# A fourth gate product with a wide moving operand, wide matmuls ahead of narrow ones, and eight slots traded for four wide buffers

## The chip, the cores and the metric

The kernel runs on one core of a Trainium2 chip. The metric is the device time of one execution in microseconds. Three runs of the kernel before took 1026.03, 1027.26 and 1027.35 us (median 1027.26).

## The reference

A decoder trunk of two layers on 512 tokens of width 1024 in float32. The first layer mixes with a gated short convolution, the second with sliding-window attention over one shared K/V; both end in a gated FFN of width 2816, and every part has a norm ahead and behind.

```python
def swiglu(h, w_gate_up, w_down):
    g, u = jnp.split(h @ w_gate_up, 2, axis=-1)
    return (jax.nn.silu(g) * u) @ w_down
...
kv = rmsnorm(h, kv_norm) @ w_kv
q = (rmsnorm(h, b_pre_norm[j]) @ b_w_q[j]).reshape(bsz, s, N_HEADS, HEAD_DIM)
attn = sliding_window_sink_attention(q, k_sh, v_sh, b_sinks[j]) @ b_w_o[j]
h = h + rmsnorm(attn, b_post_norm[j])
ff = swiglu(rmsnorm(h, ffn_pre_norm[l]), ffn_w_gate_up[l], ffn_w_down[l])
h = h + rmsnorm(ff, ffn_post_norm[l])
```

Attention has 16 heads of 64, 4 K/V heads, blocks of 128 queries that see their own and the previous block, and a sink logit per head.

## The kernel before, in words

**Precision.** Every float32 operand is kept as a rounded part (names ending in hi, made by ACT) and a rest (lo, made by DVE as the operand minus its rounded part). A product is three matmuls: hi times lo, hi times hi, lo times hi (`mm3`, L190 to L193). A weight tile of 128x1024 arrives by DMA as `raw`, ACT makes `whi` (L469), DVE makes `wlo` (L470); `in_line` (from L474) prepares them two jobs ahead of the job that uses them.

**Gate stage of an FFN.** `gate_jobs` (from L976) computes the gate and up projections of two feature tiles by seven block products in place of eight, in Strassen's manner, 10 groups of features per layer. The sums of token blocks are made once per layer in `factors` (L364), those of weight blocks by DMA accumulation or, for 6 of the 10 groups (`ADDED`), partly by DVE at L457. The products of a group run in the order 1, 2, 6, 5, 7, 3, 4. Products 1, 6, 7, 4 accumulate in one chain, X, of two banks (one for each half e of the outputs); 5 and 3 in chain Z, 2 in chain Y. After each product `take` (from L1001) copies or adds the banks into the buffers `st` and `u`.

For products 6, 7 and 4 the token factor `xt` is one wide buffer, its rounded part in columns 0 to 511 and its rest in 512 to 1023. A view of both pieces (256 columns of each) is one moving operand of 512 columns: one wide matmul (L1048) makes hi times hi into the bank's left half and hi times lo into its right half, and a narrow one (L1050, 256 columns) adds lo times hi on the left. They alternate: wide, narrow, wide, narrow, over e and k. The right half is added later by DVE (L1008). Product 1 takes the token tiles 0 to 3 themselves, whose two parts lie in separate slots, so it has three narrow matmuls per step and only a left half.

**Buffers.** One ring of 43 slots (`slot`: 128x512) and one of 14 wide buffers (`wide`: 128x1024) hold everything that is not a weight. `halves` gives the two halves of a wide buffer. A slot is handed out again in order; whoever writes its new tile waits for the last reader of the old one. Weights have 7 raw and 4 pairs of rounded buffers of their own.

**Order.** All four engines run what is written, in the order written (`manual_schedule`). In the attention stage the table `ORDER` sets it: per pair of heads t it interleaves scores, maxima, exponents, turning (transposing probabilities on PE), high (`phi`, ACT, L1369) and low (`plo`, DVE, L1373) parts of turned blocks, weighing (PE, `po`), the output `out` (L1389 to 1391), and the projection and rotation of the next heads' queries (`ra`, `rhi`, `rlo` at L1241, L1246, L1247; additions on POOL, which is GpSimd, for most). Scores, turned parts and rotated queries all live in slots. Ahead of it stands the projection of K and V from `xkv`, whose eight token tiles are split by `Update.split` (L338), as are the FFN's. An `Update` can have several sets of tiles n: the K/V update has n = 0 (for K and V) and n = 1 (for the queries), the FFN's only n = 0.

Of the kernel before, what the change touches and what calls it, by code (L numbers as in the profile page):

```python
# [11 lines left out]
F32R = mybir.dt.float32r  # L12
# [4 lines left out]
P = 128  # L17
D = 1024
S = 512
KT = D // P  # L20
# [31 lines left out]
    "L": "low", "W": "weigh", "O": "out", "Q": "project", "R": "rotate", "H": "split",  # L52
    "G": "weights", "Z": "project", "z": "out",
}
N_SLOT, N_WIDE, N_RAW, N_W = 43, 14, 7, 4
EARLY = 4
HD = 64
NH = 16
# [14 lines left out]
def yoco_kernel(  # L73
# [22 lines left out]
    nc = tc.nc  # L96
# [142 lines left out]
    class Update:  # L239
# [3 lines left out]
        def __init__(self, mix, gain, gpres):  # L243
            self.mix, self.gpres, self.gain = mix, gpres, gain
            self.s, self.v, self.r = (
                small.tile([P, n], F32, tag=tag, name=name(tag))
                for tag, n in (("us", 12), ("uv", 8), ("ur", 8))
            )
            self.x = [[None] * KT for _ in gpres]
            self.xn, self.banks, self.parts = {}, {}, {}  # L250
            self.leaves = False

        def load(self, queue=nc.sync):
# [82 lines left out]
                                        ident)  # L336

        def split(self, n, f, hf):  # L338
            if self.x[n][f] is None:
                self.x[n][f] = (slot("xhi", F32R), slot("xlo", F32R))  # L340
            hi, lo = self.x[n][f]
            c = slice(hf * 256, (hf + 1) * 256)
            src = self.banks[f % 4, hf][:, (f // 4) * 256 : (f // 4 + 1) * 256]
            nc.scalar.activation(hi[:, c], src, AF.Copy, scale=g(self.gpres[n], f))
            nc.vector.scalar_tensor_tensor(
                out=lo[:, c], in0=src, scalar=g(self.gpres[n], f), in1=hi[:, c].bitcast(F32),
                op0=ALU.mult, op1=ALU.subtract,
            )
# [15 lines left out]
        def factors(self):  # L364


            x = self.x[0]
            made = {p: [] for p in range(1, 8)}
            for p, k0, c in ((1, 0, 0), (2, 4, 0), (3, 4, 256)):
                made[p] = [[a[:, c : c + 256] for a in x[k0 + k]] for k in range(4)]  # L370
            for j in range(2):
                q11, q21, q12, q22 = (self.parts[i, hf, j] for hf in range(2) for i in range(2))

                nc.vector.tensor_tensor(out=q11, in0=q11, in1=q12, op=ALU.subtract)
                nc.vector.tensor_tensor(out=q12, in0=q22, in1=q12, op=ALU.subtract)
# [13 lines left out]
            return made  # L389
# [565 lines left out]
    def ffn(l, before, ahead, gain, gpres, following):  # L955
# [20 lines left out]
        def gate_jobs(q, factors, out, to, then):  # L976
# [24 lines left out]
            def take(p):  # L1001
                x, y, z = (banks.get(c) for c in "XYZ")
                st, u, gr = kept
                g0, g1 = (gr.rearrange("p (e h c) -> p e h c", e=2, h=2)[:, :, h]
                          for h in range(2))

                def add(out, a, b):
                    nc.vector.tensor_tensor(out=out, in0=a, in1=b, op=ALU.add)  # L1008

                if p == 2:  # L1010
                    add(g0, tiles(y), tiles(st))
                elif p == 5:
                    nc.scalar.activation(u, z, AF.Copy)
                elif p == 3:
                    add(g1, tiles(z), tiles(st))
                else:
                    for e in range(2):
                        a, b = x[e][:, :256], x[e][:, 256:]
                        ste, ue = (v[:, e * 256 : (e + 1) * 256] for v in (st, u))
                        if p == 7:  # L1020
# [3 lines left out]
                        nc.scalar.activation(ste, a, AF.Copy)  # L1024
                        if p != 1:
                            add(ste, b, ste)
                if p == 4:
                    for g, m in ((g0, st), (g1, u)):
                        nc.vector.scalar_tensor_tensor(out=g, in0=tiles(m), scalar=-1.0, in1=g,
                                                       op0=ALU.mult, op1=ALU.mult)  # L1030

            def run(p):
                def products(job):
# [5 lines left out]
                    if opened:  # L1039
                        banks[c] = ([bank("gx", pools[c]) for _ in range(2)] if c == "X"  # L1040
                                    else bank("g" + c.lower(), pools[c]))
                    for e in range(2):
                        for k in range(4):
                            kk = slice(e * S + k * P, e * S + (k + 1) * P)
                            xhi, xlo, *xboth = factors[p][k]
                            kw = {"skip_group_check": True}
                            if c == "X" and xboth:
                                nc.tensor.matmul(banks[c][e], whi[:, kk], xboth[0], start=False,  # L1048
                                                 stop=False, **kw)
                                nc.tensor.matmul(banks[c][e][:, :256], wlo[:, kk], xhi,  # L1050
                                                 start=False, stop=k == 3 and p == 4, **kw)
                                continue
                            out = (banks[c][e][:, :256] if c == "X"
                                   else banks[c][:, e * 256 : (e + 1) * 256])
                            mm3(out, whi[:, kk], wlo[:, kk], xhi, xlo,
                                opened and k == 0 and (c == "X" or e == 0),
                                e == 1 and k == 3 and p in (2, 3), **kw)
                    take(p)
                return products
# [213 lines left out]
    class Heads:  # L1273
# [343 lines left out]
```

## Time and profile before

| | |
|---|---|
| runs | 1026.03, 1027.26, 1027.35 us |
| profiled execution | 1026.46 us, of which span 1024.7 us |
| granted clock of PE | 0.999 |
| DVE add of a bank half (L1008) | 420 ns, 160 times |
| weight rounding on ACT (L469), rest on DVE (L470) | 1051 and 1227 ns, 225 times each |

In a timeline row the first number is the start in us from the span's start, the second the duration, then engine, line, operation, output and inputs, shape and count; a bracket gives the idle time of the engine ahead of it and what ended it. Matmuls are pipelined, so their durations overlap, and distances between starts say how fast the stream runs. A group row ends in busy time, mean of one in ns, and idle time ahead.

### The profile page before, as it was taken

To read this page: it belongs to the slowest core of one execution; us is meant where nothing else is said; L and a number is where in the kernel's file an instruction comes from. 1 tells how busy PE (TensorE), PEld (TensorE's weight loads), DVE (VectorE), ACT (ScalarE), POOL (GpSimd) and SP (SyncE) were. 2 spreads that over 40 slices of the span, in tenths; PEclk is the share of its full clock that TensorE was granted. 3 is DMA by queue.
4 is the path that set the end of the run, shared out by engine and by line. 5 is a ranking of instruction groups with operands and counts; after the bars stand their busy time and mean duration, and the time that the engine had idled before them with its cause. 6 is when DMAs were issued, how large, how long until landed. Compare 5 with 4: busy or idle time off the path is not lost.

```text
span 1024.7 us, 16538 instructions
## 1 busy us (share of the span) xinstructions
PE 1015.1 (99%) x6168; PEld 900.3 (88%) x6168; DVE 858.7 (84%) x1440; ACT 582.3 (57%) x1035; POOL 196.9 (19%) x259
## 2 busy tenths in 40 slices
PE   9999999999999999999999999999999999999997
PEld 8888888999889898998897888889998998989986
DVE  5766767889789988989869998778997898889896
ACT  7323445865655454666476776677666554645641
POOL 0443033112111111000123653232111010110001
PEclk9999999999999999999999999999999999999999
DMA  9897689459979699879504779976899576998742
GB/s 357 288 266 225 184 255 350 136 167 292 348 238 296 195 305 307 267 210 318 170 5 160 187 229 277 254 264 153 270 289 328 167 245 226 299 298 249 240 149 82
DMA packets 66576, 244.52 MB, mean 239 GB/s; under 512 B 7872, under 2 KB 8384, under 8 KB 54720
## 3 DMA queue, kind: packets, MB, share of 16 engines
q1 hardware_dynamic: 51328, 145.98, 38.9%
q0 software_dynamic: 14592, 96.48, 36.9%
q8 instruction: 48, 0.79, 0.3%
q10 hardware_dynamic: 576, 1.02, 0.3%
q14 instruction: 32, 0.26, 0.1%
HBM read 237.15 MB, written 102.76 MB: 332 GB/s over the span
## 4 chain that ended last, share of the span: by engine, by line
PE 85%; DVE 8%; ACT 2%; DMA 2%; issue 2%; POOL 0%; DVEq 0%; ACTq 0%
PE gx L1048 10%; PE gx L1050 5%; PE pcub L191 4%; PE pcub L192 4%; PE pcub L193 4%; PE gz L193 3%; PE gz L192 3%; PE gz L191 3%; PE px L191 3%; PE px L193 3%; PE px L192 3%; PE pmix L191 2%; PE pmix L192 2%; PE pmix L193 2%; DMA raw<-in_w_gb_dram 2%; PE gy L193 2%
## 5 line engine op out<-in xcount | busy, mean ns | idle before, releaser
L470 DVE TENSOR_TENSOR wlo<-raw,whi 128x1024 fp32r<-128x1024 f32 x225 | 274.8, 1227 | 64.5 <-ACT whi L469 64.1
L469 ACT ACTIVATE whi<-raw 128x1024 fp32r<-128x1024 f32 x225 | 234.0, 1051 | 104.8 <-DVE raw L457 22.3
L1048 PE MATMUL gx<-xt,whi 128*128 128x512 f32 x480 | 172.5, 399 | 0.1
L1050 PE MATMUL gx<-xt,wlo 128*128 128x256 f32 x480 | 135.0, 281 | 0.0
L1048 PEld LDWEIGHTS gx<-xt,whi 128*128 128x128 f32 x480 | 90.4, 188 | 19.7 <-DVE st L1008 0.3
L538 POOL DMA_DIRECT2D hsum<-in_w_gb_dram x96 | 63.7, 751 | 143.9 <-ACT whi L469 82.6
L1050 PEld LDWEIGHTS gx<-xt,wlo 128*128 128x128 f32 x480 | 90.9, 189 | 0.1
L1024 ACT ACTIVATE st<-gx 128x256 f32<-128x256 f32 x120 | 43.0, 379 | 63.1 <-PE gx L1050 47.8
L538 POOL DMA_DIRECT2D hsum<-hsum x32 | 25.3, 790 | 258.9 <-ACT whi L469 192.0
L1008 DVE TENSOR_TENSOR st<-gx,st 128x256 f32<-128x256 f32 x160 | 62.9, 420 | 4.3 <-ACT st L1024 2.9
L192 PE MATMUL pcub<-xhi,whi 128*128 128x512 f32 x168 | 65.4, 389 | 0.0
L191 PE MATMUL pcub<-xlo,whi 128*128 128x512 f32 x168 | 65.4, 389 | 0.0
L193 PE MATMUL pcub<-xhi,wlo 128*128 128x512 f32 x168 | 65.4, 389 | 0.0
L1062 ACT ACTIVATE gr<-gr 128x1024 f32<-128x1024 f32 x20 | 21.3, 1065 | 49.2 <-DVE gr L1008 49.2
L191 PE MATMUL px<-wlo,ahi 128*128 128x512 f32 x120 | 46.8, 390 | 0.1
L192 PE MATMUL px<-whi,ahi 128*128 128x512 f32 x120 | 46.7, 389 | 0.0
L193 PE MATMUL px<-whi,alo 128*128 128x512 f32 x120 | 46.7, 389 | 0.0
L193 PE MATMUL gz<-xhi,wlo 128*128 128x256 f32 x160 | 45.4, 284 | 0.0
L191 PE MATMUL gy<-xlo,whi 128*128 128x256 f32 x160 | 45.3, 283 | 0.0
L192 PE MATMUL gy<-xhi,whi 128*128 128x256 f32 x160 | 45.3, 283 | 0.0
L193 PE MATMUL gy<-xhi,wlo 128*128 128x256 f32 x160 | 45.3, 283 | 0.0
L192 PE MATMUL gx<-xhi,whi 128*128 128x256 f32 x160 | 45.3, 283 | 0.0
(265 smaller groups left out, 3064.5 us busy)
## 6 DMA issues: line engine op xcount, KB each, us to landing
hsum<-in_w_gb_dram POOLq DMA_DIRECT2D x96, 512.0 KB, 7.9
raw<-hsum SPq DMA_DIRECT2D x88, 512.0 KB, 7.6
raw<-in_w_gb_dram SPq DMA_DIRECT2D x60, 512.0 KB, 7.6
hsum<-in_w_dn_dram POOLq DMA_DIRECT2D x36, 512.0 KB, 8.8
raw<-in_w_dn_dram SPq DMA_DIRECT2D x32, 512.0 KB, 6.0
hsum<-hsum POOLq DMA_DIRECT2D x28, 512.0 KB, 5.9
raw<-in_w_in_dram SPq DMA_DIRECT2D x21, 512.0 KB, 7.8
hsum<-in_w_dn_dram POOLq DMA_DIRECT2D x12, 768.0 KB, 12.8
```

Source lines behind the costliest of these rows:

```text
L191: nc.tensor.matmul(out, whi, xlo, start=start, stop=False, **kw)
L192: nc.tensor.matmul(out, whi, xhi, start=False, stop=False, **kw)
L193: nc.tensor.matmul(out, wlo, xhi, start=False, stop=stop, **kw)
L469: self.begun = nc.scalar.activation(hi[:, :n], raw, AF.Copy)
L470: nc.vector.tensor_tensor(out=lo[:, :n], in0=raw, in1=hi[:, :n].bitcast(F32), op=ALU.subtract)
L538: nc.gpsimd.dma_start(dst, src, max_dma_last_dim=4 * 4 * S, **kw))
L1008: nc.vector.tensor_tensor(out=out, in0=a, in1=b, op=ALU.add)
L1024: nc.scalar.activation(ste, a, AF.Copy)
L1048: nc.tensor.matmul(banks[c][e], whi[:, kk], xboth[0], start=False, stop=False, **kw)
L1050: nc.tensor.matmul(banks[c][e][:, :256], wlo[:, kk], xhi, start=False, stop=k == 3 and p == 4, **kw)
L1062: nc.scalar.activation(kept[2], kept[2], AF.Silu)
```

## The change

Three things, in one edit.

1. **Product 1 with a wide operand.** `Update.split` puts token tiles 0 to 3 of set n = 0 in wide buffers; the view of both pieces goes to `factors` as a third entry of product 1. Product 1 then runs as 6, 7 and 4 do, and `take` adds its right half on DVE as well.
2. **Order in a job of chain X.** All 8 wide matmuls (both e, four k) come first, then all 8 narrow ones.
3. **Pools.** 35 slots and 18 wide buffers. The first four token tiles of the convolution, those of K/V and of both FFNs, and the first four outputs of attention move to halves of wide buffers.

```diff
-N_SLOT, N_WIDE, N_RAW, N_W = 43, 14, 7, 4
+N_SLOT, N_WIDE, N_RAW, N_W = 35, 18, 7, 4
+BOTH = 4
...
         def split(self, n, f, hf):
+            if self.x[n][f] is None and n == 0 and f < BOTH:
+                two = wide("xhl", F32R)
+                self.x[n][f] = two[:, :S], two[:, S:]
+                self.both[f] = two.rearrange("p (i c) -> p i c", i=2)
             if self.x[n][f] is None:
                 self.x[n][f] = (slot("xhi", F32R), slot("xlo", F32R))
...
             for p, k0, c in ((1, 0, 0), (2, 4, 0), (3, 4, 256)):
-                made[p] = [[a[:, c : c + 256] for a in x[k0 + k]] for k in range(4)]
+                made[p] = [[a[:, c : c + 256] for a in x[k0 + k]]
+                           + [two[:, :, c : c + 256] for two in self.both[k0 + k :][:1] if two]
+                           for k in range(4)]
...
-    xs = [(slot("xhi", F32R), slot("xlo", F32R)) for _ in range(KT)]
+    xs = [halves("xhl", F32R) if k < BOTH else (slot("xhi", F32R), slot("xlo", F32R))
+          for k in range(KT)]
...
                         nc.scalar.activation(ste, a, AF.Copy)
-                        if p != 1:
-                            add(ste, b, ste)
+                        add(ste, b, ste)
...
-                    for e in range(2):
-                        for k in range(4):
-                            kk = slice(e * S + k * P, e * S + (k + 1) * P)
-                            xhi, xlo, *xboth = factors[p][k]
-                            kw = {"skip_group_check": True}
-                            if c == "X" and xboth:
-                                nc.tensor.matmul(banks[c][e], whi[:, kk], xboth[0], start=False,
-                                                 stop=False, **kw)
-                                nc.tensor.matmul(banks[c][e][:, :256], wlo[:, kk], xhi,
-                                                 start=False, stop=k == 3 and p == 4, **kw)
-                                continue
...
+                    if c == "X":
+                        for e, k, kk in steps:
+                            nc.tensor.matmul(banks[c][e], whi[:, kk], factors[p][k][2],
+                                             start=opened and k == 0, stop=False, **kw)
+                        for e, k, kk in steps:
+                            nc.tensor.matmul(banks[c][e][:, :256], wlo[:, kk], factors[p][k][0],
+                                             start=False, stop=k == 3 and p == 4, **kw)
...
         def out(self):
-            hi, lo = slot("ohi", F32R), slot("olo", F32R)
+            if self.t < BOTH:
+                hi, lo = halves("ohl", F32R)
+            else:
+                hi, lo = slot("ohi", F32R), slot("olo", F32R)
```

PE has 160 matmuls fewer, DVE 40 additions more.

**PE, end of product 4 of one gate group and start of product 1 of the next** (`gx` is a bank of chain X, `xt` a token factor, `xhi`, `xlo` and `xhl` token tiles). Before:

```order
1114 L1048 MATMUL gx_2024<-xt_1899,whi_2150 128x512
1115 L1050 MATMUL gx_2024<-xt_1899,wlo_2151 128x256
1116 L1048 MATMUL gx_2024<-xt_1915,whi_2150 128x512
1117 L1050 MATMUL gx_2024<-xt_1915,wlo_2151 128x256
1118 L1048 MATMUL gx_2024<-xt_1915,whi_2150 128x512
1119 L1050 MATMUL gx_2024<-xt_1915,wlo_2151 128x256
1120 L191 MATMUL gx_2255<-xlo_1633,whi_2180 128x256
1121 L192 MATMUL gx_2255<-xhi_1632,whi_2180 128x256
1122 L193 MATMUL gx_2255<-xhi_1632,wlo_2181 128x256
```

The same place in the change; "x2" stands for two such rows in a row, with different columns of the weight tile:

```order
1080 L1055 MATMUL gx_2015<-xt_1891,whi_2136 128x512 x2
1081 L1055 MATMUL gx_2015<-xt_1907,whi_2136 128x512 x2
1082 L1055 MATMUL gx_2016<-xt_1891,whi_2136 128x512 x2
1083 L1055 MATMUL gx_2016<-xt_1907,whi_2136 128x512 x2
1084 L1058 MATMUL gx_2015<-xt_1891,wlo_2137 128x256 x2
1085 L1058 MATMUL gx_2015<-xt_1907,wlo_2137 128x256 x2
1086 L1058 MATMUL gx_2016<-xt_1891,wlo_2137 128x256 x2
1087 L1058 MATMUL gx_2016<-xt_1907,wlo_2137 128x256 x2
1088 L1055 MATMUL gx_2241<-xhl_1628,whi_2166 128x512
1089 L1055 MATMUL gx_2241<-xhl_1631,whi_2166 128x512
```

The wide ones of both banks now stand ahead of the narrow ones, and product 1 begins with wide matmuls on `xhl`.

**DVE, around the start of a gate group** (`wlo` a weight's rest, `a_...` and `s_...` of pair sums for the down projection, `st` the group's buffer). Before:

```order
246 L470 TENSOR_TENSOR wlo_2246<-raw_2000,whi_2245 128x1024 [waits Activation_49]
247 L470 TENSOR_TENSOR wlo_2284<-raw_2008,whi_2283 128x1024 [waits PE_49,Activation_49]
248 L581 TENSOR_TENSOR a_456_2251<-gr_2022,a_456_2251 128x256 [waits Activation_49]
249 L1008 TENSOR_TENSOR gr_2254<-gy_2291,st_2252 128x2x256 [waits PE_49]
250 L470 TENSOR_TENSOR wlo_2318<-raw_2055,whi_2317 128x1024 [waits DMAHW6_49,Activation_49]
```

In the change:

```order
248 L478 TENSOR_TENSOR wlo_2232<-raw_1992,whi_2231 128x1024 [waits Activation_49]
249 L1017 TENSOR_TENSOR st_2238<-gx_2241,st_2238 128x256 [waits Activation_49]
250 L1017 TENSOR_TENSOR st_2238<-gx_2242,st_2238 128x256 [waits Activation_49]
251 L478 TENSOR_TENSOR wlo_2264<-raw_2000,whi_2263 128x1024 [waits Activation_49]
252 L589 TENSOR_TENSOR a_448_2237<-gr_2014,a_448_2237 128x256 [waits Activation_49]
253 L1017 TENSOR_TENSOR gr_2240<-gy_2271,st_2238 128x2x256 [waits DVE_49,PE_49]
```

Two additions per group stand between the rests of two weights, and each waits for ACT's copy of the left half.

**DVE and ACT in the attention stage, second and third pair of heads** (`pt` a bank of turned probabilities, `lp` a fixed last block, `se` sums, `ra`, `rhi` rotated queries). The names behind "waits" are the engines whose semaphores the row waits for. DVE before, then in the change:

```order
751 L1237 STREAM_SHUFFLE sh_6138<-pk_5285 128x512
752 L1239 TENSOR_TENSOR ra_6140<-pk_5285,ctab_5288 128x512
753 L1373 TENSOR_TENSOR plo_6083<-pt_6077,phi_6082 128x512 [waits Activation_49,Pool_49]
754 L1373 TENSOR_TENSOR lp_5620<-pt_6113,lp_5619 128x2x128 [waits Activation_49]
755 L1339 TENSOR_TENSOR se_6105<-se_6105,rs_6106 128x4
```

```order
771 L1244 STREAM_SHUFFLE sh_6065<-pk_5213 128x512 [waits PE_49]
772 L1246 TENSOR_TENSOR ra_6067<-pk_5213,ctab_5216 128x512 [waits DVE_49,PE_49]
773 L1380 TENSOR_TENSOR plo_6010<-pt_6004,phi_6009 128x512 [waits DVE_49,PE_49,Activation_49]
774 L1380 TENSOR_TENSOR lp_5548<-pt_6040,lp_5547 128x2x128 [waits Activation_49]
775 L1346 TENSOR_TENSOR se_6032<-se_6032,rs_6033 128x4
```

The order is the same; the rest `plo` now waits for PE, namely for the matmul that reads the block ahead of it. ACT before, then in the change:

```order
492 L1246 ACTIVATE rhi_6144<-ra_6140 128x512 [waits Pool_49]
493 L1390 ACTIVATE ohi_6217<-po_6148 128x512 [waits PE_49]
494 L1369 ACTIVATE phi_6201<-pt_6196 128x512 [waits PE_49,Activation_49]
495 L1369 ACTIVATE phi_6226<-pt_6221 128x512 [waits PE_49]
496 L186 ACTIVATE whi_6281<-raw_6279 128x1024 [waits DMAHW4_49]
```

```order
490 L1253 ACTIVATE rhi_6071<-ra_6067 128x512 [waits PE_49,Pool_49]
491 L1400 ACTIVATE ohl_6144<-po_6075 128x512 [waits PE_49]
492 L1376 ACTIVATE phi_6128<-pt_6123 128x512 [waits PE_49]
493 L1376 ACTIVATE phi_6152<-pt_6147 128x512 [waits PE_49,Pool_49]
494 L187 ACTIVATE whi_6207<-raw_6205 128x1024 [waits DMAHW6_49]
```

The second `phi` of the pair now also waits for POOL, whose rotation sum still uses the slot's old tile; the next `phi` but one has a wait for POOL as well.

More of the change, by code (lines that the diff above doesn't have):

```diff
@@ L250, in __init__ @@
             self.xn, self.banks, self.parts = {}, {}, {}
+            self.both = [None] * KT
             self.leaves = False
@@ L1041, in products @@
                                     else bank("g" + c.lower(), pools[c]))
-                    for e in range(2):
-                        for k in range(4):
-                            kk = slice(e * S + k * P, e * S + (k + 1) * P)
-                            xhi, xlo, *xboth = factors[p][k]
-                            kw = {"skip_group_check": True}
-                            if c == "X" and xboth:
-                                nc.tensor.matmul(banks[c][e], whi[:, kk], xboth[0], start=False,
-                                                 stop=False, **kw)
-                                nc.tensor.matmul(banks[c][e][:, :256], wlo[:, kk], xhi,
-                                                 start=False, stop=k == 3 and p == 4, **kw)
-                                continue
[L1053 to L1056, printed above, removed]
+                    steps = [(e, k, slice(e * S + k * P, e * S + (k + 1) * P))
+                             for e in range(2) for k in range(4)]
+                    kw = {"skip_group_check": True}
+                    if c == "X":
[6 more added lines that the diff above has]
+                    else:
+                        for e, k, kk in steps:
+                            mm3(banks[c][:, e * 256 : (e + 1) * 256], whi[:, kk], wlo[:, kk],
+                                *factors[p][k][:2], opened and e == k == 0,
                                 e == 1 and k == 3 and p in (2, 3), **kw)
@@ L1388, in out @@
         def out(self):
-            hi, lo = slot("ohi", F32R), slot("olo", F32R)
+            if self.t < BOTH:
+                hi, lo = halves("ohl", F32R)
+            else:
+                hi, lo = slot("ohi", F32R), slot("olo", F32R)
             nc.scalar.activation(hi, self.po, AF.Copy)
```

## The prediction

> **What bounds the kernel now.** I read the span and the busy shares first, then the chain of work that ended last, then the groups of instructions by cost.
>
> ```profile
> span 1024.7 us, 16538 instructions
> PE 1015.1 (99%) x6168; PEld 900.3 (88%) x6168; DVE 858.7 (84%) x1440; ACT 582.3 (57%) x1035; POOL 196.9 (19%) x259
> PE 85%; DVE 8%; ACT 2%; DMA 2%; issue 2%; POOL 0%; DVEq 0%; ACTq 0%
> ```
>
> PE (TensorE) is busy 99% of the span and holds 85% of the chain; DVE (VectorE) holds 8%. So a cheaper matmul stream is worth what it saves, and an edit off PE costs only where DVE or ACT (ScalarE) already ends a wait of PE. Two stretches answer where that is:
>
> ```profile
> 225.00:490.00 265.00, 264.83 (x1666) 239.49 (x1665) 234.51 (x339) 151.83 (x219) 31.14 (x47) 1.00 0.86 272
> 545.00:610.00 65.00, 64.13 (x426) 52.55 (x426) 63.19 (x195) 46.87 (x142) 37.20 (x38) 1.00 0.68 182
> ```
>
> The columns are the stretch, its length, then busy time of PE, weight loads, DVE, ACT and POOL. In the first FFN (225 to 490) PE idles 0.17 us while DVE has 30.5 us of idle time: PE sets the time. In the early attention heads (545 to 610) DVE has only 1.81 us idle of 65 and PE 0.87: there a delay of DVE is almost a delay of the kernel. The profiled run took 1026.46 us, 1.76 more than its span and 0.80 below the median of 1027.26. I make the sum against 1026.46.
>
> **Gate products: the matmul stream.** The groups touched are these:
>
> ```profile
> L1048 PE MATMUL gx<-xt,whi 128*128 128x512 f32 x480 | 172.5, 399 | 0.1
> L1050 PE MATMUL gx<-xt,wlo 128*128 128x256 f32 x480 | 135.0, 281 | 0.0
> L192 PE MATMUL gx<-xhi,whi 128*128 128x256 f32 x160 | 45.3, 283 | 0.0
> L1008 DVE TENSOR_TENSOR st<-gx,st 128x256 f32<-128x256 f32 x160 | 62.9, 420 | 4.3 <-ACT st L1024 2.9
> L1024 ACT ACTIVATE st<-gx 128x256 f32<-128x256 f32 x120 | 43.0, 379 | 63.1 <-PE gx L1050 47.8
> ```
>
> Product 1 takes 160 steps of three narrow matmuls now; they become one wide and one narrow. Products 6, 7 and 4 have 480 pairs of a wide and a narrow, alternating; they keep their count and are regrouped. The means (399, 281, 283 ns) overlap, so they don't price a step; the distance from start to start does. In these rows from the timeline of PE the first number is the start:
>
> ```profile
> 303.98 0.40 PE L1048 MATMUL gx<-xt,whi 128*128 128x512 f32 x1
> ...
> 306.45 0.40 PE L1048 MATMUL gx<-xt,whi 128*128 128x512 f32 x1
> 306.69 0.28 PE L1050 MATMUL gx<-xt,wlo 128*128 128x256 f32 x1
> 306.81 0.28 PE L191 MATMUL gz<-xlo,whi 128*128 128x256 f32 x1
> 309.68 0.40 PE L1048 MATMUL gx<-xt,whi 128*128 128x512 f32 x1
> 59.74 0.39 PE L191 MATMUL pcub<-xlo,whi 128*128 128x512 f32 x1
> 65.18 0.39 PE L191 MATMUL pcub<-xlo,whi 128*128 128x512 f32 x1
> ```
>
> From 303.98 to 306.81 stand 8 alternating pairs: 2.83/8 = 354 ns a pair. From 306.81 to 309.68 stand 24 narrow matmuls: 120 ns each, 360 for three. From 59.74 to 65.18 stand 24 plain 512-wide ones: 226.7 each. So a pair taken apart should cost 226.7 + 120 = 346.7, and the alternation shows 7.3 ns more. If the excess belongs to the alternation, grouping removes it; if it belongs to the wide operand (two pieces 512 columns apart, which no plain stream here has), it stays. No row separates these. Ends: product 1 saves 160 x (360 - 354) = 1.0 us to 160 x (360 - 346.7) = 2.1 us; grouping saves 0 to 480 x 7.3 ns = 3.5 us. I take half the excess as removable, 3.3 us together (1.5 + 1.8), with the ends 1.0 and 5.6. A loss of PE by the order alone I exclude: plain streams of each width run at 226.7 and 120 ns, no slower than in alternation.
>
> The Trainium skill, "TensorE: Matmul & The Clock Gate", section "Back-to-back issue gap", puts an isolated gap at N/2.4 + 2.5 ns, whatever the neighbours. That would be 325 ns for wide plus narrow and 328 for three narrow: an estimate of 0.4 us for product 1, and nothing for the order. The trace's 226.7 and 120 ns are above it and differ from each other in another ratio, so the sum goes by the trace.
>
> **Gate products: the additions.** Product 1 now leaves two halves in its banks, so DVE adds the second half twice per group of output columns: 40 more adds at 420 ns (750 ns the pair). In most groups the DVE idle of the first FFN takes them. In the 6 of 10 groups per layer for which DVE also makes sums of raw weights it doesn't quite; the first row is such a group's window, with 10.79 of 11.50 us of DVE busy:
>
> ```profile
> 225.70:237.20 11.50, 11.50 (x86) 10.89 (x85) 10.79 (x19) 6.94 (x12) 2.96 (x4) 1.00 0.60 133
> ...
> 233.99 0.75 DVE L1008 TENSOR_TENSOR st<-gx,st 128x256 f32<-128x256 f32 x2
> 235.41 0.40 PE L1048 MATMUL gx<-xt,whi 128*128 128x512 f32 x1
> 421.89 0.75 DVE L1008 TENSOR_TENSOR st<-gx,st 128x256 f32<-128x256 f32 x2
> 422.36 0.50 PE L1048 MATMUL gx<-xt,whi 128*128 128x512 f32 x1
> ```
>
> Product 7 overwrites the banks that product 6's adds read. They end at 234.74, 0.67 us before it starts; 0.75 us more on DVE ahead of them eats that and 0.08 us beyond. At 421.89 the adds are late already: the wide matmul follows the last narrow one, which started at 421.94, after 0.42 instead of 0.12 us. There the extra pair costs most of its time, which I put at 0.5 us. So 12 groups at about 0.1 and that one: 1.7 us. Ends: 0, if DVE's idle takes all, and 12 x 0.3 (the one wait seen) + 0.75 = 4.4. ACT's first copy of a job comes after 8 wide and 4 narrow matmuls instead of 4 pairs, by 8 x 234 + 4 x 120 - 4 x 354 about 0.9 us later; ACT's idle (63.1 us before these copies) covers it, and the second copy, which ends the job, does not move. Net for the gates: -3.3 + 1.7, about -1.6 us, ends +3.4 and -5.6; by its nearest rows I call it -1.5.
>
> **The pools: slots for wide buffers.** The bytes are the same, 43 slots of 512 and 14 wide of 1024 against 35 and 18. But 8 of the 16 token slots of the K/V projection are now halves of wide buffers. When that projection ends, 8 slots come free for the heads, not 16, while a head's tiles (probabilities, rotated queries, their rounded parts and rests) all draw on slots. So the ring turns sooner, and a tile's writer now waits for the reader of an earlier one. The order of instructions shows three such waits that the profile of before says are late:
>
> ```profile
> 579.54 0.68 DVE L1373 TENSOR_TENSOR plo<-pt,phi 128x512 fp32r<-128x512 f32 x1
> 581.14 0.28 PE L191 MATMUL po<-plo,vt 128*128 128x256 f32 x1
> 585.72 0.60 ACT L1369 ACTIVATE phi<-pt 128x512 fp32r<-128x512 f32 x1 [0.98 <-PE pt L1356]
> 587.94 1.28 POOL L1241 TENSOR_TENSOR ra<-ra,sh 128x512 f32<-128x512 f32 x1
> 587.95 0.40 ACT L1327 ACTIVATE s<-s,nm 128x128 f32<-128x128 f32 x1 [0.68 <-DVE nm L1311]
> 590.72 0.60 ACT L1369 ACTIVATE phi<-pt 128x512 fp32r<-128x512 f32 x1
> 590.80 1.70 POOL L1247 TENSOR_TENSOR rlo<-ra,rhi 128x512 fp32r<-128x512 f32 x1 [0.85 <-ACT rhi L1246]
> 592.87 0.68 DVE L1373 TENSOR_TENSOR plo<-pt,phi 128x512 fp32r<-128x512 f32 x1
> ```
>
> First, the rest of the turned probabilities (plo, third block of a head) must wait for the weighing matmul that reads the block before it; that one ends at 581.42, so DVE starts 1.88 us late. Behind it on DVE stand the other rest, the row sums, the reciprocals and the scaling, and the chain of before runs over exactly these to PE's transposes:
>
> ```profile
> 579.62 0.60 DVE plo L1373
> 581.77 1.64 DVE s L1344 x3
> 583.45 0.59 PE pt L1356 x3
> ```
>
> So 1.85 us reach PE. Second, the next head's phi on ACT, 585.72, must wait for POOL's rotation sum, which ends at 587.94 + 1.28 = 589.22: 3.50 us. Behind it ACT holds a weight rounding, four exponentials and rhi; ACT's one idle piece there is 0.68 us, so they come 2.8 us late. POOL's rlo waits for rhi (its row says so) and comes as late, ending near 595.3; and third, the phi of 590.72 must now wait for that rlo. Then plo at 592.87, again on the chain, starts at about 595.9, 3.0 us late. DVE has a little idle of its own between, so I take 2.7. Together **+4.5 us**. Ends: +1.9, if slack that I don't see absorbs all behind the first (with DVE's 1.81 us of idle taken as well, about 0), and 1.88 + 3.50 + 1.78 = 7.2, where all three are paid in full. A gain I exclude: no tile of the heads finds its slot free earlier. Other new waits fall on engines that have time.
>
> **The start.** Token tiles in wide buffers let ACT round a first-stage weight ahead of the last square, and two more ahead of dhi.
>
> ```profile
> L469 ACT ACTIVATE whi<-raw 128x1024 fp32r<-128x1024 f32 x225 | 234.0, 1051 | 104.8 <-DVE raw L457 22.3
> 27.80 0.69 DVE L723 TENSOR_TENSOR dlo<-dg,dhi 128x512 fp32r<-128x512 f32 x1
> L724 PE MATMUL pr<-dlo,ones_r x1: 392/392/392, 32.7 to 32.7; 128*128 128x512 f32 x1
> ```
>
> dlo is ready at 28.5 and its reader starts at 32.7: 4.2 us of cover, against three roundings of 1.05 us. I cost it at 0 (ends 0 and 0.7).
>
> **The sum.** 1026.46 + 4.5 - 1.5 = 1029.5. The median of before lies 0.80 above the profiled run; half of that goes on top, since one profiled run is no better a centre than three timed ones: 1030.0.
>
> **The rivals.**
> *The order buys nothing.* The 7.3 ns are the two-piece operand's. A sign for it: in the last alternating pair the narrow step takes 306.69 to 306.81, the 120 ns of a plain narrow stream, so the excess sits in the wide step (240 ns by the rows, 354 - 120 = 234 by the mean). Then PE gains 1.0 us, the adds cost 1.7, the waits 4.5: 1026.46 + 5.2 + 0.4 = 1032. This is also the skill's side (0.4 in place of 1.0 us).
> *The waits hide.* Only the first is paid, at 1.9: 1026.46 + 1.9 - 1.5 + 0.4 = 1027.3. For it speaks that PE runs projections for later heads beside the waits; against it DVE's 63.19 of 65 us.
> *Faster.* One mechanism: grouped wide matmuls run at the plain 226.7 ns, so the 640 pairs save 5.6 us, of which the adds take 1.7. It decides once the attention waits cost under 1.8 us: with the first paid at 1.3, 1026.46 - 3.9 + 1.3 + 0.4 = 1024.3. Against it stands that the excess sits in the wide step.
> *The change does not do what it says.* Product 1 is called wide, yet three narrow (360) and a pair (354) cost nearly the same on PE; its whole gain of 1.0 us may go to 40 adds on DVE. This is contained in the first rival.
>
> **How the numbers follow.** A measurement of this kernel can tell about 0.2%, 2.05 us, from no change: 1025.2 and 1029.3 are the borders. Chances: forecast (1028 to 1031.5) 0.47, order buys nothing 0.15, waits hide 0.22, faster 0.16. The forecast's lower part lies within the border, so same gets 0.22 and some 0.08 of it, slower the rest. Range 1024.5 to 1033.5: it takes in the centres of all cases but the last's, and 1026.46 + 7.2 of attention in full less the gate gain; about 2 in 10 is left out.
>
> **What would show it.** Right: starts of grouped wide matmuls 227 to 232 ns apart; in the attention stage DVE idle before plo ended by PE, ACT idle before phi ended by POOL, PE idle of 545 to 610 up from 0.87 by 3 to 5 us, and PE's later stages shifted by that. Wrong: grouped wide steps at 234 ns, PE idle in that stretch unchanged, or PE waits for DVE's st at the gates of more than 2 us.

## The result, and the profile after

The changed kernel takes 1030.24 us (median of 6 runs, 1029.12 to 1031.69) against 1026.51 us before (median of 6, 1025.71 to 1027.35). The ratio is 1.0036, with a 95% interval of 1.0026 to 1.0046: 3.7 us slower.

The page of the changed kernel, busy shares and chain:

```profile
span 1027.3 us, 16280 instructions
PE 1012.6 (99%) x6008; PEld 893.2 (87%) x6008; DVE 869.5 (85%) x1480; ACT 581.7 (57%) x1035; POOL 196.1 (19%) x259
PE 82%; DVE 8%; DMA 4%; ACT 3%; issue 2%; POOL 1%; DVEq 0%; SPq 0%; ACTq 0%; POOLq 0%
```

PE has less to do than before, 1012.6 us in place of 1015.1, and yet the span grew by 2.6 us. So PE waits more, and the two stretches say where (length, then busy time of PE, weight loads, DVE, ACT, POOL):

```profile
225.00:490.00 265.00, 264.52 (x1602) 237.15 (x1601) 241.10 (x357) 152.09 (x219) 31.05 (x47) 1.00 0.86 274
545.00:613.00 68.00, 63.34 (x424) 51.96 (x424) 61.68 (x195) 45.52 (x141) 36.86 (x38) 1.00 0.66 175
```

In the first FFN PE idles 0.48 us in place of 0.17. In the attention heads it idles 4.66 us in place of 0.87. What it waits for there is told by the view of PE's waits in the heads: who waits for whom, us in total, how often, the longest. First before, from 545 to 610:

```profile
PE psc L1299 <- DVE nm L1311: 0.6, 2, 0.3
```

Then the changed kernel, from 545 to 613:

```profile
PE psc L1306 <- DVE nm L1318: 1.9, 1, 1.9
PE po L192 <- DVE plo L1380: 1.8, 2, 1.2
PE pt L1363 <- DVE s L1351: 0.8, 1, 0.8
```

0.6 us became 4.5. The same stretch by rows, in the timelines of PE, DVE, ACT and POOL; the bracket is the idle time ahead and what ended it:

```profile
580.28 0.28 PE L192 MATMUL po<-plo,vt 128*128 128x256 f32 x1
580.66 0.69 DVE L1380 TENSOR_TENSOR plo<-pt,phi 128x512 fp32r<-128x512 f32 x1 [1.42 <-issue]
581.40 0.39 PE L192 MATMUL po<-plo,vt 128*128 128x256 f32 x1 [0.60 <-DVE plo L1380]
584.35 0.33 PE L1363 MATMUL pt<-ident,s 128*128 128x128 f32 x1 [0.84 <-DVE s L1351]
589.20 0.60 ACT L1376 ACTIVATE phi<-pt 128x512 fp32r<-128x512 f32 x1 [3.88 <-POOL ra L1248]
593.54 1.29 POOL L1254 TENSOR_TENSOR rlo<-ra,rhi 128x512 fp32r<-128x512 f32 x1 [3.65 <-ACT rhi L1253]
594.86 0.60 ACT L1376 ACTIVATE phi<-pt 128x512 fp32r<-128x512 f32 x1 [1.47 <-POOL rlo L1254]
595.49 0.69 DVE L1380 TENSOR_TENSOR plo<-pt,phi 128x512 fp32r<-128x512 f32 x1 [1.87 <-ACT phi L1376]
596.24 0.39 PE L192 MATMUL po<-plo,vt 128*128 128x256 f32 x1 [1.21 <-DVE plo L1380]
604.47 0.76 PE L1306 MATMUL psc<-rlo,rhi 64*128 64x256 f32 x2 [1.87 <-DVE nm L1318]
```

Read it from the top. The rest `plo` comes late on DVE, and PE's weighing (`po`) and transposing (`pt`) with it. The view names no releaser of that wait ("issue"); the weighing matmul that the prediction named is the first row here, and it ends at 580.56, 0.10 us ahead of `plo`. So that PE ends this wait is read from the order of instructions and the times, not from the bracket. ACT then stands 3.88 us in front of a `phi` until POOL's rotation sum has ended; before, it stood 0.98 us there, for PE. POOL's `rlo` idles 3.65 us for ACT's `rhi`, which stood behind that `phi`; the next `phi` waits for that `rlo`; and PE waits twice more, 1.21 and 1.87 us. No row of before has a `phi` that waits for POOL at these places.

To place gains and losses I line up the same matmul in two profiles and subtract its start in the profile of before. These shifts in us, at places told by before's time, serve all versions below:

| kernel | at 203 us | at 490 (first FFN over) | at 560 (heads begin) | at 620 | at 700 (second FFN begins) | at 897 | at 1016 |
|---|---|---|---|---|---|---|---|
| changed | +0.50 | -0.77 | -0.82 | +2.97 | +2.95 | +1.75 | +1.85 |
| changed, second profile (`again`) | -0.08 | -2.08 | -2.12 | +1.67 | +1.67 | +0.45 | +2.42 |
| `pools_only` | +0.70 | +0.30 | +0.27 | +4.06 | +4.06 | +4.06 | +4.57 |
| `order_only` | +0.49 | -0.35 | -0.40 | -0.46 | -0.44 | -1.12 | -0.73 |
| `no_adds` | -0.06 | -2.28 | -2.32 | +1.42 | +1.43 | +0.10 | +0.95 |
| `relief` | +0.77 | -0.96 | -1.01 | -1.07 | -1.07 | -2.29 | -1.79 |
| `relief_third` | -0.04 | -2.18 | -2.22 | -1.50 | -1.50 | -2.70 | -2.40 |
| `p1_only` | -0.03 | +2.12 | +2.09 | +1.99 | +1.96 | +1.49 | +2.12 |
| `mixed` | +0.75 | -0.37 | -0.40 | -0.48 | -0.48 | -1.34 | -1.45 |
| `held` | +0.41 | +0.37 | +0.32 | +5.72 | +5.72 | +5.72 | +5.70 |

The changed kernel loses 3.79 us between 560 and 620 in both of its profiles. The first column differs between two profiles of the same code, so it is chance.

One more difference stands behind the last matmul. From its start to the end of the span the changed kernel takes 7.88 and 7.91 us in its two profiles, before and every other version 7.05 to 7.07. It is the last store of the output, on ACT's queue; the rows end in the us from issue to landing. Before, then the changed kernel:

```profile
out_dram<-h ACTq DMA_DIRECT2D x1, 256.0 KB, 2.1
```

```profile
out_dram<-h ACTq DMA_DIRECT2D x1, 256.0 KB, 2.9
```

So 0.8 us of the loss is a store that lands later, and since both profiles have it, it is hardly chance. `relief`, `no_adds` and `pools_only` differ from the changed kernel only in places far ahead of it and have 2.1. What makes the store slower is open.

### The profile page after: what moved, and what is told of

It is laid out like the page before. It is cut to its first block, busy times and chain, and to the rows that moved or that the text cites. A ratio compares the mean times of both kernels' runs of the same rounds, so it can differ in the third digit from the quotient of the medians.

```text
span 1027.3 us, 16280 instructions
## 1 busy us (share of the span) xinstructions
PE 1012.6 (99%) x6008; PEld 893.2 (87%) x6008; DVE 869.5 (85%) x1480; ACT 581.7 (57%) x1035; POOL 196.1 (19%) x259
## 4 chain that ended last, share of the span: by engine, by line
PE 82%; DVE 8%; DMA 4%; ACT 3%; issue 2%; POOL 1%; DVEq 0%; SPq 0%; ACTq 0%; POOLq 0%
PE gx L1055 13%; PE gx L1058 7%; PE pcub L193 4%; PE pcub L192 4%; PE pcub L194 4%; DMA raw<-in_w_gb_dram 4%; PE gz L194 3%; PE gz L193 3%; PE gz L192 3%; PE px L192 3%; PE px L193 3%; PE px L194 3%; PE pmix L193 2%; PE pmix L192 2%; PE pmix L194 2%
## 5 line engine op out<-in xcount | busy, mean ns | idle before, releaser
L1055 PE MATMUL gx<-xt,whi 128*128 128x512 f32 x480 | 120.9, 394 | 0.6 <-DVE st L1017 0.6
L1055 PEld LDWEIGHTS gx<-xt,whi 128*128 128x128 f32 x480 | 86.2, 189 | 16.7 <-DVE st L1017 1.0
L1017 DVE TENSOR_TENSOR st<-gx,st 128x256 f32<-128x256 f32 x200 | 77.7, 418 | 2.4 <-ACT st L1033 0.5
L1058 PEld LDWEIGHTS gx<-xt,wlo 128*128 128x128 f32 x480 | 65.5, 190 | 4.7
L1058 PE MATMUL gx<-xt,wlo 128*128 128x256 f32 x480 | 66.9, 282 | 0.0
L192 PE MATMUL gz<-xt,whi 128*128 128x256 f32 x160 | 45.3, 283 | 0.0
L193 PE MATMUL gz<-xt,whi 128*128 128x256 f32 x160 | 45.3, 283 | 0.0
L192 PE MATMUL gz<-xlo,whi 128*128 128x256 f32 x160 | 45.3, 283 | 0.0
L193 PE MATMUL gz<-xhi,whi 128*128 128x256 f32 x160 | 45.3, 283 | 0.0
```

Of the source, the lines that this page charges most:

```text
L192: nc.tensor.matmul(out, whi, xlo, start=start, stop=False, **kw)
L193: nc.tensor.matmul(out, whi, xhi, start=False, stop=False, **kw)
L1055: nc.tensor.matmul(banks[c][e], whi[:, kk], factors[p][k][2], start=opened and k == 0, stop=False, **kw)
L1058: nc.tensor.matmul(banks[c][e][:, :256], wlo[:, kk], factors[p][k][0], start=False, stop=k == 3 and p == 4, **kw)
```

## The experiments

The theory: fewer free slots for the first heads make three writers wait, and that is the loss; grouping the matmuls gains, since alternation costs. The rivals: the loss is at the gates (the 40 additions), or something in the wide tiles.

### The order alone (`order_only`)

On the kernel before, products 6, 7 and 4 only:

```diff
...
+                    if c == "X" and p != 1:
+                        for e, k, kk in steps:
+                            nc.tensor.matmul(banks[c][e], whi[:, kk], factors[p][k][2],
+                                             start=False, stop=False, **kw)
+                        for e, k, kk in steps:
+                            nc.tensor.matmul(banks[c][e][:, :256], wlo[:, kk], factors[p][k][0],
+                                             start=False, stop=k == 3 and p == 4, **kw)
...
```

> The kernel before, with only the order changed: in products 6, 7 and 4 all 8 wide matmuls first, then all 8 narrow ones. Theory (alternation costs, grouping takes most of it away): a job of 16 goes from 2.83 to 2.79 us as in the changed kernel, 60 jobs, so 2 to 2.4 us faster, ratio about 0.998; attention as before. Rival (the wide operand in two pieces costs, whatever the order): 0 to 0.3 us. A loss would speak for ACT's later first copy.

1024.31 us (median of 11) against 1026.24: ratio 0.9985, 0.9976 to 0.9993. (Here and below the ratio is to runs of the kernel before that were taken with the version.) A job in its timeline of PE, from the first wide matmul to the job behind it:

```profile
304.14 2.00 PE L1047 MATMUL gx<-xt,whi 128*128 128x512 f32 x8
305.99 1.11 PE L1050 MATMUL gx<-xt,wlo 128*128 128x256 f32 x8
306.94 0.28 PE L191 MATMUL gz<-xlo,whi 128*128 128x256 f32 x1
```

306.94 - 304.14 = 2.80 us in place of 2.83, and 1.85/8 = 231 ns a wide step. Grouping alone is a gain, as the theory has it. But the wide steps don't fall to 227 ns at once: the medians of the eight, over the 60 jobs, are 233, 236, 228, 232, 231, 227, 227 and 227 ns.

### One piece in place of two (`one_piece`)

```diff
-                    made[p] += [[hi[:, c : c + 256], lo[:, c : c + 256], two[:, :, c : c + 256]]
+                    made[p] += [[hi[:, c : c + 256], lo[:, c : c + 256], hi]
```

> The kernel before, alternating, but the wide operand of products 6, 7 and 4 is 512 neighbouring columns (the rounded part of both halves of the tokens) instead of two pieces 512 apart; so hi times lo is replaced by a product of other tokens. Theory (alternation costs): a pair still takes 352 to 354 ns, a job 2.82 to 2.83 us. Rival (the two-piece operand costs): 347 ns a pair, 2.77 us a job.

```profile
304.20 0.40 PE L1048 MATMUL gx<-xt,whi 128*128 128x512 f32 x1
...
307.03 0.28 PE L191 MATMUL gz<-xlo,whi 128*128 128x256 f32 x1
```

Eight alternating pairs with an operand of 512 neighbouring columns take 2.83 us, the same as with two pieces; the one execution took 1026.38 us. So the two pieces are not the reason. Grouping takes away 4.9 of the excess of 7.3 ns a pair (2.832 - 2.793 us over 8 pairs), and that part belongs to the alternation; the other 2.4 ns stay in the first wide steps of a group, and why is open.

### The buffers alone (`pools_only`)

The changed kernel with the gate loop, the factors and `take` of before; pools and halves as changed:

```diff
-                        add(ste, b, ste)
+                        if p != 1:
+                            add(ste, b, ste)
...
-                           + [two[:, :, c : c + 256] for two in self.both[k0 + k :][:1] if two]
```

> The changed kernel's buffers (35 slots, 18 wide, token tiles and attention outputs in halves of wide ones) with the gate code of before: three narrow matmuls in product 1, alternating order, no 40 additions. Theory (fewer slots in attention make plo and phi wait): PE's stage from 545 to 610 us gets 3.5 to 4.0 us longer and the whole 3.5 to 4.5 us slower than before, the worst of all versions. Rival (the loss comes from the 40 additions or the order at the gates): within 0.5 us of before.

1031.00 us (median of 5), ratio 1.0050, 1.0038 to 1.0063: the slowest but one of all versions, without any change at the gates. PE's waits in its attention stage are those of the changed kernel:

```profile
PE psc L1307 <- DVE nm L1319: 1.9, 1, 1.9
PE po L192 <- DVE plo L1381: 1.8, 2, 1.2
PE pt L1364 <- DVE s L1352: 0.8, 1, 0.8
```

The whole loss comes with the buffers, +3.79 us between 560 and 620 once more.

### The additions (`no_adds`)

```diff
-                        add(ste, b, ste)
+                        if p != 1:
+                            add(ste, b, ste)
```

> The changed kernel without the 40 DVE additions of product 1's right half; it leaves out rounded weight times token rest of product 1. Theory (additions cost little, about 1 us in the groups with sums of raw weights): 0.5 to 1.2 us faster than the changed kernel, 2.5 to 3.5 slower than before, and the jobs of 2.90 us where DVE is late go back to 2.79. Rival (the additions are what slows): 3 us or more faster than the changed kernel, at or under the time of before.

1028.67 us (median of 11), ratio 1.0022, 1.0013 to 1.0031. That is 1.1 to 1.6 us under the changed kernel's two medians, but the intervals of the ratios overlap. At like clock the distance is wider: where the granted clock was 0.998 or 0.999, the four executions average 1027.3 us and the changed kernel's seven 1029.4; where it was 0.996 or 0.997, seven average 1029.3 and five 1031.0. Of these 1.7 to 2.1 us the slower last store can be 0.8; 0.9 to 1.3 are left. The shifts show less. From 700 to 897 us it gains 1.33 us, the changed kernel 1.20 and 1.22: 0.1 us for the additions of that stretch. In the first FFN it gains 2.22, the changed kernel 1.27 and 2.00. Six jobs of products 6, 7 and 4 are about 0.1 us longer than the rest in the changed kernel (five in its second profile), one in before and one in `no_adds`: some 0.5 us. The rival, 3 us or more, is out.

### Wide buffers for the heads (`relief`) and for one pair only (`relief_third`)

```diff
-                phi, plo = slot("phi", F32R), slot("plo", F32R)
+                phi, plo = (halves("phl", F32R) if self.t < BOTH
+                            else (slot("phi", F32R), slot("plo", F32R)))
```

> The changed kernel, but the turned probabilities phi and plo of the first four head pairs are halves of wide buffers instead of slots, so that no writer meets an occupied slot; all the arithmetic is the same. Theory (slot waits in attention are the loss): PE's stage from 545 to 610 is as long as before, 3.5 to 4 us faster than the changed kernel, and 0.5 to 2 us faster than before, since the gates keep their gain. Rival (the waits are a by-product of another delay there): as slow as the changed kernel, with the same idle time of PE in attention.

1024.81 us (median of 11), ratio 0.9983, 0.9974 to 0.9992. PE's waits in attention are back to one short kind, and the heads lose nothing (-1.01 to -1.07):

```profile
PE psc L1306 <- DVE nm L1318: 0.5, 2, 0.3
```

The second version has `self.t == 2` in place of `self.t < BOTH`.

> The changed kernel with phi and plo of the third head pair alone in wide buffers. By the order of waits this leaves the first late writer (plo near 580 us behind PE) and removes the two on ACT behind POOL. Theory (the losses add up in two steps): the idle stretches of PE before 585 us stay (0.60 and 0.84 us), those of 1.21 and 1.87 us near 596 and 604 go; 2.5 to 3 us faster than the changed kernel, about 0.5 us on either side of before. Rival (the first wait is the cause of the later ones): all four stay or shrink alike, at most 1 us faster.

Its view of PE's waits in attention:

```profile
PE pt L1363 <- DVE s L1351: 0.8, 1, 0.8
PE po L192 <- DVE plo L1381: 0.6, 1, 0.6
PE psc L1306 <- DVE nm L1318: 0.3, 1, 0.3
```

As the theory has it, the two stretches of the first late writer stay (0.6 and 0.8), those of 1.21 and 1.87 are gone. The first costs 0.72 us between 560 and 620, so the other two cost 3.79 - 0.72 = 3.07. The time came out lower than I expected: 1024.52 us (median of 11), ratio 0.9980, 0.9971 to 0.9989, over 5 us under the changed kernel and as good as `relief`. The trace accounts for 3.1 of it in attention and for 0.8 in the last store. Part of the rest is the clock: 5 of the 12 executions of the changed kernel had a granted clock of 0.996 or 0.997, none of the 11 of `relief_third` and of the 11 of `relief` had one under 0.998 (more below, at `again`). What remains is about 1 us and open.

### The same shortage without the change (`held`)

On the kernel before, four slots taken after K/V and given back later:

```diff
+        hold = [slot("hold") for _ in range(4)]
+        for h in hold:
+            nc.gpsimd.memset(h[:, :1], 0.0)
...
+            if i == 3:
+                for h in hold:
+                    nc.gpsimd.memset(h[:, :1], 0.0)
```

> The kernel before with nothing changed at the gates or the pools; four slots are taken (one column of each set on POOL) after the K/V projection and given back after the third pair of heads. Theory (a shortage of free slots in the first heads is the whole loss): the same late writers come back without any other part of the change, plo and phi wait for PE and POOL at 579 to 592 us, and the whole is 2.5 to 4 us slower than before. Rival (the wide tiles themselves or their dependencies cost): within 0.5 us of before.

1031.58 us (median of 5), ratio 1.0053, 1.0038 to 1.0067. The shortage alone makes the loss, and more of it than expected: PE's waits add up to only 3.0 us, 2.4 more than before, yet the heads lose 5.40:

```profile
PE psc L1299 <- DVE nm L1311: 1.8, 1, 1.8
PE pt L1356 <- DVE s L1344: 1.2, 2, 0.8
```

The rest is PE's clock. These are 512-wide matmuls of query projections:

```profile
587.34 0.77 PE L191 MATMUL pq<-xlo,whi 128*128 128x512 f32 x1
587.91 0.63 PE L192 MATMUL pq<-xhi,whi 128*128 128x512 f32 x1
588.34 0.63 PE L193 MATMUL pq<-xhi,wlo 128*128 128x512 f32 x1
588.76 0.63 PE L191 MATMUL pq<-xlo,whi 128*128 128x512 f32 x1
```

and the rows of that stretch, in which the column behind POOL's is the granted clock:

```profile
586.00:588.00 2.00, 2.00 (x18) 1.77 (x17) 2.00 (x7) 0.50 (x1) 0.32 (x1) 0.72 0.55 115
588.00:590.00 2.00, 2.00 (x6) 1.56 (x5) 2.00 (x9) 0.00 (x0) 1.92 (x2) 0.50 0.00 0
590.00:592.00 2.00, 2.00 (x13) 1.43 (x13) 1.48 (x5) 1.65 (x3) 1.03 (x2) 0.93 0.59 66
```

The starts are 427 ns apart in place of 227, at a granted clock of 0.50. The three rows miss 0.28, 0.50 and 0.07 of 2 us each, 1.70 us in all, or 3.4 us at half clock. It happens a second time, from 607 to 611, with another 1.70 us (0.59 and 0.56 in two such rows). The two drops come 1.4 and 1.7 us behind the ends of idle stretches of PE of 0.83 and 1.84 us. With the 2.4 us of waits that makes 5.8, so 0.4 of it did not reach the end of the heads.

### Parts and a mixture (`p1_only`, `mixed`) and a second profile (`again`)

`p1_only` is `relief` with wide and narrow alternating:

```diff
                             nc.tensor.matmul(banks[c][e], whi[:, kk], factors[p][k][2],
                                              start=opened and k == 0, stop=False, **kw)
-                        for e, k, kk in steps:
                             nc.tensor.matmul(banks[c][e][:, :256], wlo[:, kk], factors[p][k][0],
```

> Product 1 wide, phi and plo of the first four pairs in wide buffers (so without the slot waits), but wide and narrow alternate as before. Theory: 160 steps gain 6 ns each, 1.0 us, and the 40 additions give back about 1.6 us, so 0 to 1 us slower than before, and 2 us slower than the same kernel with grouped order. Rival (the wide product is the gain and the order a detail): 1 to 2 us faster than before.

1026.00 us (median of 11), ratio 0.9997, 0.9988 to 1.0006: no change that can be told, between the two expectations. (Its profile is that of its slowest execution, 1028.57 us; it has two waits of PE, 1.6 us at 290 and 1.0 at 419, to which it owes its +2.12 in the table.) From 700 to 897 us, away from disturbances, it gains 0.47, `order_only` 0.68, and both together 1.22 (`relief`): the two gains add, and the order is the larger one.

`mixed` is `relief` with product 1 wide only where DVE makes no sums of raw weights:

```diff
-                        add(ste, b, ste)
+                        if p != 1 or q not in ADDED:
+                            add(ste, b, ste)
...
-                    if c == "X":
+                    if c == "X" and not (p == 1 and q in ADDED):
```

> The version with phi and plo in wide buffers, grouped order, and product 1 wide only in the 4 of 10 groups per layer in which DVE makes no sums of raw weights (three narrow matmuls and no addition elsewhere). Theory (the additions cost only where DVE is nearly full): the saving of 8 groups, 0.09 us each, stays and the cost of the additions goes, 0.3 to 1.0 us faster than with product 1 wide everywhere, about 1024 us. Rival (the additions cost everywhere alike): no difference to it beyond 0.2 us.

1024.40 us (median of 11), ratio 0.9979, 0.9971 to 0.9988. It is 0.4 under `relief`, within the intervals: not decided.

`again` is the changed kernel without an edit.

> The changed kernel once more, unchanged, for a second profile. Theory (after PE idles near 604 us its clock drops in some executions): executions fall near 1029.2 us with a granted clock of 0.998, or 2 us higher with 0.996 to 0.997; a profile of the second kind has 512-wide matmuls 427 ns apart for about 2.5 us after an idle stretch. Rival (the spread comes from DMA at the start and in the gate stage): the upper executions have the same clock, and the difference stands before 500 us.

1029.76 us (median of 6), ratio 1.0032, 1.0021 to 1.0044. Neither side is wholly right. Over the 12 executions of the two sets, the 5 with a granted clock of 0.996 or 0.997 took 1029.8 to 1031.7 us, the 7 with 0.998 or 0.999 took 1028.4 to 1031.0; the averages are 1031.0 and 1029.4. One drop as in `held`, 1.70 us, lowers the mean clock of such a run by 0.0017, so one in each of the five fits both the clock and the 1.6 us; no profile of such an execution was kept, so that is not shown. The profile of this set was not of the first kind; it lost 1.9 us elsewhere, between 897 and 985, behind late DMA. ACT's roundings of that place:

```profile
910.67 1.06 ACT L477 ACTIVATE whi<-raw 128x1024 fp32r<-128x1024 f32 x1 [4.86 <-DMA raw<-hsum]
915.65 1.06 ACT L477 ACTIVATE whi<-raw 128x1024 fp32r<-128x1024 f32 x1 [3.92 <-DMA raw<-in_w_gb_dram]
```

So the spread goes with the clock and with late DMA.

## Why the prediction was right, step by step

**What bounds the kernel.** Right: PE's saving counted in the gate stages, and the delay of DVE and ACT counted in the heads.

**The matmul stream, -3.3 us.** Nearly right, somewhat low. A job of product 1 in the changed kernel:

```profile
292.60 1.98 PE L1055 MATMUL gx<-xhl,whi 128*128 128x512 f32 x8
294.41 1.12 PE L1058 MATMUL gx<-xhl,wlo 128*128 128x256 f32 x8
...
295.36 0.28 PE L192 MATMUL gy<-xlo,whi 128*128 128x256 f32 x1
```

295.36 - 292.60 = 2.76 us; over the 20 jobs the mean is 2.785 in place of 2.875, so 1.8 us (1.5 predicted). The 60 jobs of 6, 7 and 4 have a median of 2.793 in place of 2.832: 2.3 us (1.8 predicted), or 4.9 of the 7.3 ns a pair. The prediction left open whether the excess was the alternation's, and leaned on the wide step's 234 ns as a sign for the operand; `one_piece` shows that the sign misled: with one piece the pair takes as long. Why the wide step is the long one is not shown; a narrow one ahead of it isn't the whole reason, since in groups wide steps behind wide ones take up to 236 ns.

**The additions, +1.7 us.** Too high by the traces, not settled by the times. The traces give them 0.1 us from 700 to 897 us, where five of the second FFN's six groups with sums of raw weights stand, and some 0.5 in all. So "12 groups at about 0.1" failed: it took every place where DVE is nearly full for one where PE waits. The times leave them 0.9 to 1.3 us (`no_adds` at like clock), and `relief`, which has product 1's gain of 1.8 us and the additions, is no faster than `order_only`, which has neither. The last figure of these rows is PE's wait for `st` ahead of wide matmuls, in the changed kernel:

```profile
L1055 PE MATMUL gx<-xt,whi 128*128 128x512 f32 x480 | 120.9, 394 | 0.6 <-DVE st L1017 0.6
```

and in `no_adds`, with no additions for product 1:

```profile
L1056 PE MATMUL gx<-xt,whi 128*128 128x512 f32 x480 | 120.3, 392 | 0.8 <-DVE st L1017 0.8
```

It is no longer with them, but it stands elsewhere. Near 915 us, in the changed kernel's second profile, product 6 waits for the new additions of product 1:

```profile
923.79 0.75 DVE L1017 TENSOR_TENSOR st<-gx,st 128x256 f32<-128x256 f32 x2
924.26 2.14 PE L1055 MATMUL gx<-xt,whi 128*128 128x512 f32 x8 [1.01 <-DVE st L1017]
```

In `no_adds` product 7 of the same group waits for those of product 6:

```profile
928.20 0.75 DVE L1017 TENSOR_TENSOR st<-gx,st 128x256 f32<-128x256 f32 x2
928.67 2.11 PE L1056 MATMUL gx<-xt,whi 128*128 128x512 f32 x8 [0.82 <-DVE st L1017]
```

In both DVE is late there already. What makes it late, near 420 and 915 us, are late raw weights: the changed kernel's two profiles gain 1.2 us each from 700 to 897, and one of them gives 1.9 back by 985. That the DMA is the cause of it is read from the waits, not tried.

**Attention, +4.5 us.** The mechanism was right to the rows, and the sum a little high: 3.79 in both profiles. `plo` starts 1.94 us later than before's, counted from the shift of -0.82 (1.88 predicted). Of the two steps, the first was mis-sized: 1.85 us were said to reach PE; 0.60 + 0.84 reached it, and half of that came back within the stage, 0.3 us of it as an old wait for `psc` that vanished (0.6, 2 times, became 0.3, once, in `relief_third`); 0.72 is left. The second, 2.7, came out at 3.1, which is what PE's waits of 1.21 and 1.87 add up to. That a shortage of slots is the cause is shown from both sides: `relief` takes the waits away and the loss with them, `pools_only` and `held` bring it without a change at the gates.

**The start, 0.** Right; the shift of +0.50 in the one profile is -0.08 in the other.

**The sum.** In the trace: +3.79 in the heads, -1.27 and -1.20 in the FFNs, chance at the start (+0.50), and 0.8 in the last store, which the prediction did not have; this profiled run took 1029.14 us, at the lower end of its set. The forecast of 1030.0 lies 0.2 us off the median, and that closeness is luck: attention and, by the traces, the additions were put too high, the matmul stream's gain too low, and the slower store and the lower clock of some executions were left out. The sign and the place of the loss were not luck.

**The rivals.** "The order buys nothing" fell with `order_only`; "the waits hide" with PE's 4.5 us; "faster" needed attention to cost under 1.8 us. `relief` is that case made true: without the waits the same gates end 1.4 us under before. The fourth, that product 1's gain may go to the additions, is not refuted: `relief` (1024.81 us) and `relief_third` (1024.52) have both and are no faster than the order alone (1024.31), and `p1_only` can't be told from before.

## What to carry to other kernels

Buffers of two sizes that add up to the same bytes are not the same pool: count what is free at the moment when the most is drawn, and look in the order of instructions for writers that now wait for a reader of another engine. The saving was there all along: `order_only`, `relief`, `relief_third` and `mixed` all end 1.4 to 2.0 us under the kernel before, and the simplest of them, eight wide matmuls ahead of eight narrow ones with nothing else changed, is as fast as any (1024.31 us). The wide product 1 added nothing that the times can tell. A late writer on an engine off the critical path need not cost what it is late: `plo`, 1.94 us late, cost 0.72 us, and in `held` 2.4 us more of PE's waits cost 5.40, because PE's clock dropped behind them.

## What the runs showed of the hardware

A matmul of 512 columns and one of 256 in alternation take 354 ns a pair, whether the wide operand is one piece or two. In groups of eight they take 349 ns (2.793 us for eight pairs), which was run with two pieces only.

PE's clock can halve after short idle stretches: in `held` 512-wide matmuls ran at 427 ns, with a granted clock of 0.50, twice for 3.4 us, behind idle stretches of 0.83 and 1.84 us. The changed kernel has an idle stretch of 1.87 us in both profiles and kept its clock there, so the length of one gap does not decide it; what does is open. The Trainium skill, "TensorE: Matmul & The Clock Gate", section "Back-to-back issue gap", has N/1.2 ns for a cold PE, which makes an estimate of 427 ns for 512 columns, and the trace's 427 ns agrees. The Trainium skill, under the same title, section "HAM oscillation — how this bites in real kernels", gives the rule of no idle gaps over some 3.4 us. Here the longest gap ahead of a drop was 1.84 us, so the measurement is the stricter, and it decides.
